# Two value projections done together, with some seven-product tile pairs, and the attention output held unsplit

## The chip, the cores and the metric

One core of one Trainium2 chip runs the whole program. The metric is the device time of one execution in microseconds (us); the time of a kernel is the median of several executions. Matrix products run on the tensor engine (PE); around it work the vector engine (DVE), the scalar engine (ACT), GpSimd (POOL) and a sync engine (SP) whose queue carries nearly all weight transfers. PE accumulates in eight banks of PSUM memory of 128 partitions x 512 floats.

## The reference

A decoder trunk on 256 tokens of width 2048, batch 1, two layers, all in float32:

```python
h = x
for layer in range(2):
    xn = rms_norm(h, attn_norm_g[layer])
    if layer == 0:                       # dilated sliding windows
        qkv = (xn @ w_qkv).reshape(b, s, 3, 3, 16, 128)   # group, q/k/v, head
        for g, (window, dilation) in enumerate(((128, 1), (512, 4), (2048, 16))):
            o_g, lse_g = window_attention(rope(q_g), rope(k_g), v_g)
        h = h + (sum_g softmax_g(lse)_g * o_g) @ w_o
    else:                                # latent attention on one shared K/V
        h = h + mla_attention(xn, k_nope, k_pe, v, ...)
    g, u = split(rms_norm(h, ffn_norm_g[layer]) @ w_gu)   # hidden width 5632
    h = h + (silu(g) * u) @ w_down
out = rms_norm(h, final_norm_g)
```

The change lies in the first layer's attention. It has 16 heads of 128; each head has a query, a key and a value for each of three groups, so the projection `w_qkv` has 2048 rows and 18432 columns. The mixture of the three groups is one softmax over the scores of all three together.

## The kernel before, in words

**Products.** A float32 product is made of three matmuls in a reduced-precision float32 form. Every operand is split into `hi` (the value rounded to that form, a copy on ACT) and `lo` (what is left, a subtraction on DVE); the product is hi x hi + hi x lo + lo x hi. Activations are held transposed, as 16 contraction tiles of 128 partitions with 256 columns of `hi` and 256 of `lo` for the tokens (`xT`). In `x_stationary` (L453) a 128-token half of x is loaded into PE and 512 columns of weights are streamed past it, three matmuls 128x512 a product. In `w_stationary` (L438) the weights are loaded and x is streamed.

**Weights.** All weights of the program are one list of units in the order of their use (`units`, from L294), mostly of 1 MB. `WeightStream` loads them through three `raw` buffers and splits each into `hi` and `lo` (three buffers each) two units ahead of the one in use: `next` (L195) issues the split of the unit two on, then loads. The forms "eight" and "seven" belong to a pair of contraction tiles times two blocks of 512 columns. Such a 2 x 2 product of blocks (two token halves x two contraction tiles x two column blocks) takes eight products; in the form "seven" it takes seven, from sums of blocks: four DVE operations on `raw` (L184 to L187) form sums of weights, split into `th` and `tl` (one buffer each), and the like sums of x are made once for all (`forms`, L655 to L664). The seven products go into the two accumulators of the column blocks and into four more banks (`pb`), which ACT and DVE join at the end (L704 to L711). Sums need x scaled by its token scale, or at least by a power of two near it, since the sums mix tokens.

**The feed-forward part** uses this for gate and up: `mixed` (L666) goes through eight pairs, of which `SEVEN = (2, 4, 6)` take seven products, except in each layer's first block of columns.

**The first attention** takes the heads in four quads. A quad projects values for its four heads, group by group, 16 products of contraction in four units each (L586; ACT takes the accumulator out with the token scale `rstd`, L590), and then, for two pairs of heads and three groups, the queries and keys (L597, two units each). `Later` (L203) holds work that is put some units ahead: scores come two units after their key (L604), and for a pair's last group the softmax of both its heads follows (L562 to L566); the values come three units after it (L605): PE transposes the softmax weights (L514), a copy brings them to `pt`, and four to six products with the values give the head's output (L572 to L578), which is split into `oT` right away (L581). So the second pair's softmax and values fall into the next quad's first value projection. A framework then orders the instructions of each engine by its own estimates, and each engine works through its list in order.

**Scales.** x is transposed with the layer's gain but without the token scale. The scale goes into the values as a column (`rstd`), into the softmax (`sc`, `nsc`), and into the keys as a row (`row_a["R"]`, L531). `across` (L423) makes such a row with one `diag` product on PE.

**Memory.** The pool `big` (L229) has two buffers of 4 MB; they hold in turn x, the transposed x (`xT_a`), the split output (`oT_a`) and the later stages' transposed activations.

## Time and profile before

| | |
|---|---|
| time, median of 3 runs | 2679.18 us (2678.85 to 2680.68) |
| profiled execution: time / span | 2679.5 us / 2677.7 us |
| mean granted PE clock | 0.999 of full |
| PE busy | 2661.3 us, 99% of the span, 12986 instructions |
| PE weight loads (overlap PE) | 2236.9 us, 84% |
| DVE busy | 1915.4 us, 72%, 2584 instructions |
| ACT busy | 1264.4 us, 47%, 1603 instructions |
| POOL busy | 5.5 us |
| read from memory | 491.57 MB, 184 GB/s over the span |

In the rows of the profile, an instruction is named by line, engine, operation and output <- inputs, with partitions x elements; a square bracket behind a row of the timeline gives the idle time of the engine just before it and what ended that. "PEld" is the loading of the stationary operand. The chain of waits is the work that ended last, followed back to the start.

### The profile page before, as it was taken

The numbers are of one execution on the slowest core, as the hardware profiler recorded it, in microseconds if no ns is written. First come the engines' busy times: TensorE is split into PE (matmuls) and PEld (weight loads), VectorE is DVE, ScalarE is ACT, GpSimd is POOL, SyncE is SP. The second block draws the span as 40 slices with busy tenths as digits, with TensorE's granted clock in tenths as the row PEclk, the third lists the DMA queues.
The fourth block names the chain that finished last, engine by engine and source line by source line (L and its number), as shares of the span: only waits on it lengthen the run. The fifth ranks groups of instructions, "written<-read, shape, count | busy, mean of one in ns | idle before, by whom it ended". The sixth has DMA issues, their size and how long they took to land.

```text
span 2677.7 us, 32660 instructions
## 1 busy us (share of the span) xinstructions
PE 2661.3 (99%) x12986; PEld 2236.9 (84%) x12986; DVE 1915.4 (72%) x2584; ACT 1264.4 (47%) x1603; POOL 5.5 (0%) x12
## 2 busy tenths in 40 slices
PE   9999999999999999999999999999999999999998
PEld 7888888888888888888888888888888888888887
DVE  5676577477467668966995796588578848984985
ACT  5444444444444445544553454565445534543553
POOL 0000000000000000000000000000000000000000
PEclk9999999999999999999999999999999999999999
DMA  7545555555555555565565655544555665655564
GB/s 272 189 160 171 189 165 168 186 173 173 173 183 164 195 182 189 189 204 189 189 219 190 204 180 197 161 140 146 174 173 189 205 198 179 219 190 194 191 217 138
DMA packets 302712, 495.78 MB, mean 185 GB/s; under 512 B 12680, under 2 KB 115808, under 8 KB 302176
## 3 DMA queue, kind: packets, MB, share of 16 engines
q1 hardware_dynamic: 301936, 492.64, 55.4%
q8 instruction: 101, 1.65, 0.3%
q10 hardware_dynamic: 624, 1.07, 0.1%
q14 instruction: 51, 0.42, 0.0%
HBM read 491.57 MB, written 2.10 MB: 184 GB/s over the span
## 4 chain that ended last, share of the span: by engine, by line
PE 95%; DVE 2%; DMA 1%; ACT 1%; issue 1%; SPq 0%; POOL 0%; POOLq 0%; DVEq 0%; ACTq 0%
PE acc L444 14%; PE acc L464 12%; PE acc L463 12%; PE acc L465 12%; PE acc L675 9%; PE acc L676 9%; PE acc L677 9%; PE acc L447 7%; PE bank L676 2%; PE bank L675 2%; PE bank L677 2%; PE bank L398 1%; PE bank L559 1%; DMA raw<-in_ffn_w_gu_dram 1%; PE bank L514 1%
## 5 line engine op out<-in xcount | busy, mean ns | idle before, releaser
L157 DVE TENSOR_TENSOR lo<-raw,hi 128x1024 fp32r<-128x1024 f32 (+2 forms) x578 | 667.5, 1179 | 464.2 <-ACT hi L156 447.9
L156 ACT CAST hi<-raw 128x1024 fp32r<-128x1024 f32 (+2 forms) x578 | 561.6, 1017 | 728.0 <-PE acc L465 312.1
L166 ACT CAST hi<-raw 128x1024 fp32r<-128x1024 f32 (+1 forms) x292 | 323.3, 1139 | 317.8 <-PE acc L677 96.3
L167 DVE TENSOR_TENSOR lo<-raw,hi 128x1024 fp32r<-128x1024 f32 (+1 forms) x292 | 383.4, 1330 | 83.5 <-ACT hi L166 82.8
L675 PE MATMUL acc<-hi,xT_f 128*128 128x512 f32 x988 | 387.2, 392 | 1.7 <-DVE gate L711 1.6
L676 PE MATMUL acc<-lo,xT_f 128*128 128x512 f32 x988 | 385.3, 390 | 0.0
L677 PE MATMUL acc<-hi,xT_f 128*128 128x512 f32 x988 | 385.2, 390 | 0.0
L444 PE MATMUL acc<-xT_a,hi 128*128 128x512 f32 x1536 | 379.3, 395 | 0.0
L444 PEld LDWEIGHTS acc<-xT_a,hi 128*128 128x128 f32 x1536 | 281.5, 188 | 53.8
L463 PE MATMUL acc<-hi,hT 128*128 128x512 f32 x704 | 274.7, 390 | 0.0
L465 PE MATMUL acc<-hi,hT 128*128 128x512 f32 x704 | 274.0, 389 | 0.0
L464 PE MATMUL acc<-lo,hT 128*128 128x512 f32 x704 | 274.0, 389 | 0.0
L675 PEld LDWEIGHTS acc<-hi,xT_f 128*128 128x128 f32 x988 | 185.5, 188 | 42.5 <-issue 2.9
L677 PEld LDWEIGHTS acc<-hi,xT_f 128*128 128x128 f32 x988 | 185.5, 188 | 39.3
L676 PEld LDWEIGHTS acc<-lo,xT_f 128*128 128x128 f32 x988 | 185.5, 188 | 38.4
L447 PEld LDWEIGHTS acc<-xT_a,lo 128*128 128x128 f32 x1536 | 196.9, 191 | 7.6
L447 PE MATMUL acc<-xT_a,lo 128*128 128x256 f32 x1536 | 199.2, 283 | 0.0
L166 ACT CAST th<-raw 128x1024 fp32r<-128x1024 f32 x120 | 121.8, 1049 | 73.1 <-DVE raw L186 64.6
L463 PEld LDWEIGHTS acc<-hi,hT 128*128 128x128 f32 x704 | 132.2, 188 | 27.6 <-issue 0.2
L465 PEld LDWEIGHTS acc<-hi,hT 128*128 128x128 f32 x704 | 132.1, 188 | 27.6
L464 PEld LDWEIGHTS acc<-lo,hT 128*128 128x128 f32 x704 | 132.2, 188 | 26.9
L464 PE MATMUL acc<-lo,xT_a 128*128 128x512 f32 x384 | 150.1, 391 | 0.8 <-DVE lo L157 0.6
(222 smaller groups left out, 3539.9 us busy)
## 6 DMA issues: line engine op xcount, KB each, us to landing
raw<-in_ffn_w_gu_dram SPq DMA_DIRECT2D x352, 512.0 KB, 4.5
raw<-in_a_w_qkv_dram SPq DMA_DIRECT2D x143, 1024.0 KB, 4.8
raw<-in_ffn_w_down_dram SPq DMA_DIRECT2D x88, 1024.0 KB, 5.1
raw<-in_a_w_o_dram SPq DMA_DIRECT2D x16, 1024.0 KB, 5.1
raw<-in_b_w_o_dram SPq DMA_DIRECT2D x16, 1024.0 KB, 5.0
raw<-in_b_w_kv_b_dram SPq DMA_DIRECT2D x8, 1024.0 KB, 5.2
raw<-in_b_w_q_b_dram SPq DMA_DIRECT2D x8, 768.0 KB, 4.8
raw<-in_b_w_q_a_dram SPq DMA_DIRECT2D x4, 1024.0 KB, 5.1
```

The costliest lines, as they stand in the source:

```text
L156: nc.scalar.copy(out=h, in_=src)
L157: nc.vector.tensor_tensor(out=l, in0=src, in1=h.bitcast(F32), op=ALU.subtract)
L166: self.nc.scalar.copy(out=hi, in_=src)
L167: self.nc.vector.tensor_tensor(out=lo, in0=src, in1=hi.bitcast(F32), op=ALU.subtract)
L444: mm(out=acc[:, i, :], lhsT=sl(hi, kk), rhs=xT[:, k0 + kk, :], start=first and kk == 0, stop=False)
L447: mm(out=acc[:, i, 0:S], lhsT=sl(lo, kk), rhs=xT[:, k0 + kk, 0:S], start=False, stop=last and kk == nk - 1)
L463: mm(out=acc[:, t, :ncol], lhsT=xh, rhs=rhs(hi, kk), start=st, stop=False)
L464: mm(out=acc[:, t, :ncol], lhsT=xh, rhs=rhs(lo, kk), start=False, stop=False)
L465: mm(out=acc[:, t, :ncol], lhsT=xl, rhs=rhs(hi, kk), start=False, stop=sp)
L675: mm(out=out, lhsT=xh, rhs=wh, start=st, stop=False)
L676: mm(out=out, lhsT=xh, rhs=wl, start=False, stop=False)
L677: mm(out=out, lhsT=xl, rhs=wh, start=False, stop=sp)
```

## The change

In quads 1, 2 and 3 the values of the first two groups are projected together by `mixed`, now a function of the whole kernel: eight units of two contraction tiles x two column blocks (one block a group), loaded by two transfers of 512 KB each in place of one of 1 MB, of which pairs 4 and 6 (`SEVEN_A`) take seven products. `mixed` returns the joined sums in `v0` and `v1`, which ACT then scales in place. Quad 0 and every third group keep their form.

For the sums, x is multiplied by a power of two of the token scale while quad 0 runs (`scaled`, eight operations in place on `xT_a`), and `rem_a`, the rest of the scale, takes the place of `rstd` behind that; the row for the keys is made a second time, from `rem_a`.

`th` and `tl` need memory in this stage too. So the two buffers of `big` become pools of their own: `big0` holds `xT_a`, and a pool `stage_a` holds x, `th` and `tl` until the attention is done; then `big1` opens. The split output has no buffer any more: heads 0 to 13 leave their output unsplit, by one ACT copy each, in the place of the untransposed x (`oT_f`), and four `output_parts` split it into the place of `xT_a` during and behind the last key product; heads 14 and 15 are split directly as before.

By the listed instructions, the program has 12667 matmuls and transposes in place of 12684: 18 fewer of 128x512, and one `diag` product more.

In the shortened `mixed`, the lines left out are those of the old one (L673 to L699) with `ga`, `ua` called `la`, `ra`.

```diff
 SEVEN = (2, 4, 6)
+SEVEN_A = (4, 6)
...
-        th, tl = [self.sum_pool.tile([P, 2048], F32R, tag=n, name=n, bufs=1) for n in ("th", "tl")]
+        th, tl = self.sum_tiles()
...
-    big = ctx.enter_context(tc.tile_pool(name="big", bufs=2))
+    bigs = [ctx.enter_context(tc.tile_pool(name="big0", bufs=1))]
...
+    stage_a = ExitStack()
+    a_pool = stage_a.enter_context(tc.tile_pool(name="stage_a", bufs=1))
+    def big_tile(i, shape, dtype, name):
+        return bigs[i].tile(shape, dtype, tag="big", name=name)
...
+    def paired(w, kp, at):
+        v = w.rearrange("(k p) c -> p k c", p=P)
+        return [v[:, 2 * kp:2 * kp + 2, b:b + 512] for b in at]
     for quad in range(HEADS // 4):
-        for g in range(NG):
+        if quad > 0:
+            at = [qkv_col(g, 2, quad * 4) for g in range(2)]
+            for kp in range(KD // 2):
+                units.append((paired(wq, kp, at), None, "seven" if kp in SEVEN_A else "eight"))
+        for g in range(NG) if quad == 0 else (2,):
...
-    xt = big_tile([P, NT, D], F32, "xt")
+    xt = a_pool.tile([P, NT, D], F32, name="xt")
+    oT_f = xt.rearrange("p t (h s) -> p (t h) s", s=S)
+    ws.sum_tiles = lambda: [a_pool.tile([P, 2048], F32R, tag=n, name=n) for n in ("th", "tl")]
...
+    def power_of_two(rstd):
+        r2, rem = [small.tile([P, NT], F32, tag=m, name=m) for m in ("r2", "rem")]
+        nc.vector.tensor_scalar(out=r2.bitcast(I32), in0=rstd.bitcast(I32), scalar1=0x7F800000,
+                                scalar2=None, op0=ALU.bitwise_and)
+        nc.vector.tensor_scalar(out=rem.bitcast(I32), in0=rstd.bitcast(I32), scalar1=0x007FFFFF,
+                                scalar2=0x3F800000, op0=ALU.bitwise_and, op1=ALU.bitwise_or)
+        return r2, rem
+    def scaled(xT, kp, R):
+        x2 = xT[:, 2 * kp:2 * kp + 2, :].rearrange("p k (h s) -> p k h s", s=S)
+        by = R.unsqueeze(1).unsqueeze(1).broadcast_to([P, 2, 2, S])
+        nc.vector.tensor_tensor(out=x2, in0=x2.bitcast(F32), in1=by, op=ALU.mult)
+    def sums(xT, kp, d):
+        x2 = xT[:, 2 * kp:2 * kp + 2, :].bitcast(F32)
+        f = tmp.tile([P, 2, S], F32, tag="t1", name="f")
+        nc.vector.tensor_tensor(out=f, in0=x2[:, :, 0:S], in1=x2[:, :, S:2 * S], op=ALU.add)
+        (a11, a21), (a12, a22) = [[f[:, k, t * P:(t + 1) * P] for t in range(NT)] for k in range(2)]
+        g = tmp.tile([P, 4, P], F32, tag="t1", name="g")
+        for i, x_, y_, op in ((0, a21, a22, ALU.add), (1, g[:, 0], a11, ALU.subtract),
+                              (2, a11, a21, ALU.subtract), (3, a12, g[:, 1], ALU.subtract)):
+            nc.vector.tensor_tensor(out=g[:, i], in0=x_, in1=y_, op=op)
+        put_split(d[:, 0], d[:, 1], g)
+    def mixed(xT, seven, forms, left, right, u2_tile):
+        la, ra = acc_tile(), acc_tile()
+        pb = None
...
+            if kp in seven:
+                i = seven.index(kp)
...
+                mul(pb[0], x(0, 0), w[:2], 1, st, sp)
...
+            later.tick()
+            if seven and kp == seven[-1]:
+                u2 = u2_tile()
+                nc.scalar.copy(out=left[:, 0], in_=pb[0])
+                for o, x_, y_ in ((u2, pb[2], left[:, 0]), (left[:, 1], pb[3], u2),
+                                  (right[:, 0], pb[1], u2), (right[:, 1], pb[1], left[:, 1])):
+                    nc.vector.tensor_tensor(out=o, in0=x_, in1=y_, op=ALU.add)
+        if not seven:
+            return la, ra
+        for acc, d in ((la, left), (ra, right)):
+            nc.vector.tensor_tensor(out=d, in0=acc, in1=d, op=ALU.add)
+        return left, right
...
     rstd = token_scale(ssq_x, "rstd")
+    r2_a, rem_a = power_of_two(rstd)
     row_a = {}
-    later.put(6, lambda: row_a.update(R=across(rstd, "R")))
+    later.put(6, lambda: row_a.update(R=across(r2_a, "R")))
     sc = small.tile([P, NT], F32, name="sc", tag="sc", bufs=1)
-    nc.vector.tensor_scalar(out=sc, in0=rstd, scalar1=P ** -0.5, scalar2=None, op0=ALU.mult)
+    nc.vector.tensor_scalar(out=sc, in0=rem_a, scalar1=P ** -0.5, scalar2=None, op0=ALU.mult)
     nsc = small.tile([P, NT], F32, name="nsc", tag="nsc", bufs=1)
-    nc.vector.tensor_scalar(out=nsc, in0=rstd, scalar1=-(P ** -0.5), scalar2=None, op0=ALU.mult)
-    oT = big_tile([P, HEADS, 2 * S], F32R, "oT_a")
+    nc.vector.tensor_scalar(out=nsc, in0=rem_a, scalar1=-(P ** -0.5), scalar2=None, op0=ALU.mult)
     swap = [(i + 16) % 32 for i in range(32)]
     with tc.tile_pool(name="attn_a", bufs=2) as ap:
         cst_a.append(ap.tile([P, C_END - C_M0], F32, name="cst_a", bufs=1))
         cos_a, sin_a = con(C_CA, S, A_ROT), con(C_SA, S, A_ROT)
+        forms_a = ap.tile([P, len(SEVEN_A), 2, 4, P], F32R, name="forms_a", bufs=1)
+        for kp in range(KD // 2):
+            later.put(7 + kp // 2, lambda kp=kp: scaled(xT, kp, row_a["R"]))
+        later.put(11, lambda: row_a.update(R=across(rem_a, "R")))
+        for i, kp in enumerate(SEVEN_A):
+            later.put(12 + i, lambda i=i, kp=kp: sums(xT, kp, forms_a[:, i]))
...
-            put_split(back(oT[:, head, 0:S]), back(oT[:, head, S:2 * S]),
-                      ot[:, :S].rearrange("p (t i) -> p t i", t=NT))
+            src = ot[:, :S].rearrange("p (t i) -> p t i", t=NT)
+            if head < HEADS - 2:
+                nc.scalar.copy(out=back(oT_f[:, head, :]), in_=src)
+            else:
+                put_split(back(oT[:, head, 0:S]), back(oT[:, head, S:2 * S]), src)
+        def output_parts(h0, h1):
+            put_split(oT[:, h0:h1, 0:S], oT[:, h0:h1, S:2 * S], oT_f[:, h0:h1, :])
         for quad in range(HEADS // 4):
-            vs = []
-            for g in range(NG):
-                acc = product(x_stationary, xT, KD)
-                v = ap.tile([P, NT, 512], F32, tag=f"v{g}", name=f"v{g}", bufs=1)
+            vs = [ap.tile([P, NT, 512], F32, tag=f"v{g}", name=f"v{g}", bufs=1) for g in range(NG)]
+            def put_v(v, acc, by):
                 for t in range(NT):
-                    nc.scalar.activation(out=v[:, t, :], in_=acc[:, t, :], func=AF.Copy, scale=rstd[:, t:t + 1])
-                vs.append(v)
+                    nc.scalar.activation(out=v[:, t, :], in_=acc[:, t, :], func=AF.Copy, scale=by[:, t:t + 1])
+            if quad > 0:
+                mixed(xT, SEVEN_A, forms_a, vs[0], vs[1],
+                      lambda: tmp.tile([P, 2, S], F32, tag="t1", name="u2").rearrange("p a b -> p (a b)"))
+                for v in vs[:2]:
+                    put_v(v, v, rem_a)
+            for g in range(NG) if quad == 0 else (2,):
+                put_v(vs[g], product(x_stationary, xT, KD), rem_a if quad > 0 or g == 2 else rstd)
             for pair in range(2):
                 st = {}
                 for g in range(NG):
                     qk = []
...
                     for which in range(2):
+                        if (quad, pair, g, which) == (HEADS // 4 - 1, 1, NG - 1, 1):
+                            oT = xT
+                            for h0 in (0, 4):
+                                later.put(1, lambda h0=h0: output_parts(h0, h0 + 4))
+                            for h0, h1 in ((8, 12), (12, HEADS - 2)):
+                                later.put(2, lambda h0=h0, h1=h1: output_parts(h0, h1))
                         acc = product(w_stationary, xT, KD, cols=(col(0), col(1)))
...
+    stage_a.close()
+    bigs.append(ctx.enter_context(tc.tile_pool(name="big1", bufs=1)))
...
+            def prepared(kp):
+                scaled(xT, kp, row["R"])
+                if kp in SEVEN:
+                    sums(xT, kp, forms[:, SEVEN.index(kp)])
             for part, (k0, n) in enumerate(FFN_PARTS):
                 last = part == len(FFN_PARTS) - 1
-                hT = big_tile([P, 16, 2 * S], F32R, "hT")
+                hT = big_tile(buf, [P, 16, 2 * S], F32R, "hT")
...
-                            later.put(kp + 3, lambda kp=kp: scaled(kp))
-                    g, u = mixed(not first, gate, up)
+                            later.put(kp + 3, lambda kp=kp: prepared(kp))
+                    g, u = mixed(xT, () if first else SEVEN, forms, gate, up,
+                                 lambda: fp.tile([P, 512], F32, tag="u2", name="u2"))
```

**First place: the start of the second quad's value projection**, where the first quad's last two heads have their softmax and values. On DVE, before, from the first head's softmax on (`sm` are the softmax weights, `sm_m` their row maxima, `sm_nb` the bias of the exponential, `sm_ri` the reciprocal of their sums, `pt` the transposed weights):

```order
L565 TENSOR_REDUCE sm_m<-mx 128x2
L157 TENSOR_TENSOR lo<-raw,hi 128x1024
L497 TENSOR_TENSOR sm_nb<-sm_m,nsc 128x2
L565 TENSOR_REDUCE sm_m<-mx 128x2
L497 TENSOR_TENSOR sm_nb<-sm_m,nsc 128x2
L504 RECIPROCAL sm_ri<-sm_rs 128x2
L506 TENSOR_SCALAR sm<-sm,sm_ri 128x512 x2
L516 COPY pt<-bank 128x512
```

The same stretch of DVE in the changed program (the rows of `raw` are the four sums of weights of pair 4):

```order
L662 TENSOR_REDUCE sm_m<-mx 128x2
L168 TENSOR_TENSOR lo<-raw,hi 128x1536
L586 TENSOR_TENSOR sm_nb<-sm_m,nsc 128x2
L662 TENSOR_REDUCE sm_m<-mx 128x2
L185 TENSOR_TENSOR raw<-raw 128x512
L586 TENSOR_TENSOR sm_nb<-sm_m,nsc 128x2
L186 TENSOR_TENSOR raw<-raw 128x512
L187 TENSOR_TENSOR raw<-raw 128x512
L593 RECIPROCAL sm_ri<-sm_rs 128x2
L188 TENSOR_TENSOR raw<-raw 128x512
L595 TENSOR_SCALAR sm<-sm,sm_ri 128x512 x2
```

Three of the four weight sums now stand ahead of the first head's reciprocal, and the fourth between it and the scaling of its weights. On PE there, before, at the transposes of the first head's weights:

```order
L463 MATMUL acc<-hi,xT_a 128x512
L514 MATMUL bank<-ident,sm 128x128 x2
L464 MATMUL acc<-lo,xT_a 128x512
L514 MATMUL bank<-ident,sm 128x128 x6
L465 MATMUL acc<-hi,xT_a 128x512
```

And in the changed program, up to the end of the transposes:

```order
L529 MATMUL acc<-hi,xT_a 128x512
L530 MATMUL acc<-lo,xT_a 128x512
L531 MATMUL acc<-hi,xT_a 128x512
L603 MATMUL bank<-ident,sm 128x128 x8
L529 MATMUL acc<-hi,xT_a 128x512
```

The eight transposes stand together, two matmuls later than the first of them stood before: 25 matmuls of the projection lie between them and the second head's scores, where it was 23.

**Second place: the end of the joint projection of groups 0 and 1**, DVE in the changed program (`u_2239` and `v_1917`, `v_1918` are the tile of the join and the two groups' values; `th`, `tl` and the `lo` ahead belong to pair 6):

```order
L168 TENSOR_TENSOR tl<-raw,th 128x1024 x2
L158 TENSOR_TENSOR lo<-raw,hi 128x1024 x3
L561 TENSOR_TENSOR u_2239<-bank,v_1917 128x512
L158 TENSOR_TENSOR lo<-raw,hi 128x1024
L561 TENSOR_TENSOR v_1917<-bank,u_2239 128x512
L561 TENSOR_TENSOR v_1918<-bank,u_2239 128x512
L561 TENSOR_TENSOR v_1918<-bank,v_1917 128x512
L565 TENSOR_TENSOR v_1917<-acc,v_1917 128x1024
L565 TENSOR_TENSOR v_1918<-acc,v_1918 128x1024
L158 TENSOR_TENSOR lo<-raw,hi 128x1024 x13
```

All of this is new here; before, DVE had nothing but `lo` rows, and the accumulators left by ACT (L590). Four `lo` of the third group's first two units stand ahead of the sums that end the join.

**Third place: the last key product of the attention**, DVE in the changed program (`qk` are keys, `sw` and `R` belong to their rotation and scale, `xT_a` is now the split output):

```order
L645 TENSOR_TENSOR qk_6948<-qk_6948,sw 32x512
L158 TENSOR_TENSOR lo<-raw,hi 128x1024
L388 TENSOR_TENSOR xT_a<-xt,xT_a 128x4x256 x2
L158 TENSOR_TENSOR lo<-raw,hi 128x1024 x2
L388 TENSOR_TENSOR xT_a<-xt,xT_a 128x4x256
L388 TENSOR_TENSOR xT_a<-xt,xT_a 128x2x256
L572 TENSOR_TENSOR qk_7046<-acc,t_7047 128x512
L158 TENSOR_TENSOR lo<-raw,hi 128x1024
L450 TENSOR_TENSOR qk_7046<-qk_7046,R 128x512
```

The four `xT_a` rows, the pieces of the output, are new; they stand ahead of the last key's evacuation (L572).

More of the change, by code (lines that the diff above doesn't have):

```diff
@@ L323, in units_ffn @@
         for k0, n in FFN_PARTS:
-            v = ffn_w_gu[layer].rearrange("(k p) c -> p k c", p=P)
             for j in range(k0, k0 + n, 4):
                 for kp in range(KD // 2):
-                    blocks = [v[:, 2 * kp:2 * kp + 2, b + j * P:b + j * P + 512] for b in (0, FF)]
-                    units.append((blocks, None, "seven" if j > 0 and kp in SEVEN else "eight"))
+                    units.append((paired(ffn_w_gu[layer], kp, (j * P, FF + j * P)), None,
+                                  "seven" if j > 0 and kp in SEVEN else "eight"))
             for c in range(0, D, 512):
```

118 lines of the change are left out of this document (39 added, 79 removed).

## The prediction

> **What bounds the kernel now.** I read the page's busy times and chain first, then the waits of the tensor engine, then the stretches of the first layer.
>
> ```profile
> span 2677.7 us, 32660 instructions
> PE 2661.3 (99%) x12986; PEld 2236.9 (84%) x12986; DVE 1915.4 (72%) x2584; ACT 1264.4 (47%) x1603; POOL 5.5 (0%) x12
> PE 95%; DVE 2%; DMA 1%; ACT 1%; issue 1%; SPq 0%; POOL 0%; POOLq 0%; DVEq 0%; ACTq 0%
> ...
> PE acc L675 <- DVE gate L711: 1.6, 2, 1.3
> ...
> 225.00:297.00 72.00, 71.99 (x338) 59.73 (x337) 37.42 (x53) 30.11 (x40) 0.00 (x0) 1.00 0.51 170
> ```
>
> PE is the bound: 95% of the chain, and its waits (microseconds in total, times, longest; the largest is shown) are crumbs. The last row is one stretch of value projections, the second quad's (length; then busy time and count for PE, PEld, DVE, ACT, POOL; the granted clock, here 1.00): PE 71.99 of 72.00, DVE 37.4. So the change is worth the PE work it removes, less any PE stall that it makes. There is no stall in that stretch to win back.
>
> **The work removed.** A pair of contraction tiles that took eight products takes seven; a product is three 128x512 matmuls. The feed-forward part does both forms already, so its rows price them:
>
> ```profile
> 1058.18 0.39 PE L675 MATMUL acc<-hi,xT_f 128*128 128x512 f32 x1
> 1063.42 0.39 PE L677 MATMUL acc<-hi,xT_f 128*128 128x512 f32 x1
> 1065.10 0.47 PE L675 MATMUL acc<-hi,xT_f 128*128 128x512 f32 x1 [1.29 <-DVE gate L711]
> 1076.99 0.39 PE L675 MATMUL bank<-hi,xT_f 128*128 128x512 f32 x1
> 1081.81 0.39 PE L675 MATMUL acc<-hi,xT_f 128*128 128x512 f32 x1
> ...
> 230.38 0.39 PE L463 MATMUL acc<-hi,xT_a 128*128 128x512 f32 x1
> 235.60 0.40 PE L465 MATMUL acc<-hi,xT_a 128*128 128x512 f32 x1
> ...
> L675 PEld LDWEIGHTS acc<-hi,xT_f 128*128 128x128 f32 x988 | 185.5, 188 | 42.5 <-issue 2.9
> ```
>
> First to last start of an eight-product tile pair is 5.24 us over 23 steps, 0.228 a matmul, so 24 take 5.47. A seven-product pair (the second block's first) runs from 1076.99 to 1081.81: 4.82. The difference is 0.65. In the first layer 24 matmuls start within 5.22 us, 0.227 each, so three are 0.68. Three quads with two such pairs each are 6 x 0.65 = 3.9 us, or 6 x 0.68 = 4.1 at best. I take 3.9.
>
> The Trainium skill ("TensorE: Matmul & The Clock Gate", section "Back-to-back issue gap") gives a stream of load and matmul pairs about 131 ns per 512-column matmul. By that 18 matmuls would be worth an estimated 2.4 us. The 0.227 of this trace decides, and the sum does not use the page's figure.
>
> **One matmul added.** The row form of the token scale is now built twice, first from the power of two, later from the rest. The trace has one such product:
>
> ```profile
> 39.34 0.39 PE L463 MATMUL acc<-hi,xT_a 128*128 128x512 f32 x1
> 40.02 0.60 PE L430 MATMUL bank<-diag,ones 128*128 128x256 f32 x2
> 41.15 0.39 PE L463 MATMUL acc<-hi,xT_a 128*128 128x512 f32 x1
> ```
>
> L463 comes every third matmul. From 39.34 to 41.15 are two threes, 6 x 0.227 = 1.36, so the product costs 0.45. The scaling of x itself is eight DVE instructions in the first quad (as L652), and the sums of each of the two tile pairs are two more of 512 columns and four of 128 (L186 has 512):
>
> ```profile
> L652 DVE TENSOR_TENSOR xT_f<-xT_f,R 128x1024 fp32r<-128x1024 f32 x16 | 19.6, 1224 | 10.9 <-PE acc L677 10.9
> L186 DVE TENSOR_TENSOR raw<-raw 128x512 f32<-128x512 f32 x60 | 41.4, 690 | 1.4
> ```
>
> At most 8 x 1.22 + 12 x 0.69 = 18 us, over eight weight tiles of 5.5 us in which the splits take two of 1.22 each: 38 of 44 us. Each scaling waits for the second group's last read of its tiles and has the length of two weight tiles until the third group's first. I put it at nothing; without that cover each late scaling would cost 1.22.
>
> **What DVE and ACT have to do more, and where.** Per quad, two weight tiles get the seven form:
>
> ```profile
> 1063.85 1.47 ACT L166 CAST hi<-raw 128x1536 fp32r<-128x1536 f32 x1 [4.07 <-PE acc L677]
> 1066.00 1.75 DVE L167 TENSOR_TENSOR lo<-raw,hi 128x1536 fp32r<-128x1536 f32 x1
> ...
> L167 DVE TENSOR_TENSOR tl<-raw,th 128x1024 fp32r<-128x1024 f32 x120 | 142.5, 1221 | 6.6 <-ACT th L166 6.2
> ```
>
> DVE: 1.75 + 4 x 0.69 + 2 x 1.22 = 6.9 us in place of 2.44, twice; then four sums of 0.69 and two of 1.22 to join the accumulators: 9.0 + 5.2 = 14 us on the 37.4 of 72. That fits on average; the place decides. The first seven-form split (pair 4) is due two tiles ahead, exactly when the preceding heads' softmax runs on DVE and ACT and PE wants its result:
>
> ```profile
> 236.03 2.00 ACT L156 CAST hi<-raw 128x1024 fp32r<-128x1024 f32 x2 [3.40 <-PE acc L465]
> 236.75 0.61 PE L559 MATMUL bank<-qk,qk 128*128 128x128 f32 x4
> 238.26 0.29 DVE L487 CUSTOM_DVE_ANT_0 sm<-bank,cst_a 128x128 f32<-128x128 f32 x1
> 239.88 0.16 DVE L497 TENSOR_TENSOR sm_nb<-sm_m,nsc 128x2 f32<-128x2 f32 x1
> 240.07 0.82 ACT L502 ACTIVATE sm<-sm,sm_nb,sc 128x512 f32<-128x512 f32 x1 [2.04 <-DVE sm_nb L497]
> 241.81 0.17 DVE L504 RECIPROCAL sm_ri<-sm_rs 128x2 f32<-128x2 f32 x1 [1.51 <-ACT sm L502]
> 242.01 0.88 DVE L506 TENSOR_SCALAR sm<-sm,sm_ri 128x512 f32<-128x512 f32 x2
> 242.55 0.44 PE L514 MATMUL bank<-ident,sm 128*128 128x128 f32 x2
> ```
>
> On this clock, with the changed order: ACT casts 1536 columns from 236.0 to 237.5. DVE, with no `lo` between the masks any more, has the second head's two (0.29 each, after the scores of 236.75) and the maximum done near 237.85, then the 1536-wide `lo` to 239.6, then the bias (0.3 earlier than now). So exp runs from 239.75, four of 0.8; its first pair ends at 241.4. But three of the four weight sums now stand ahead of the reciprocal and the fourth behind it: 239.7, 240.6, 241.3 and, after the reciprocal at 242.0, to 242.75. The first head's scaling then runs 242.75 to 243.6 instead of 242.01 to 242.89, 0.75 late. PE's transposes were put later too, behind 25 matmuls after the second scores instead of 23 (I count the order's rows), that is at 242.9. The second token half is wanted at about 243.0 and ready at 243.6: a stall of 0.6 us. Queued behind it on PE is the whole projection, so it counts in full. What follows is tight, not late: the first `pt` copy waits on ACT behind exp, `th` and the next `hi` (242.95 + 2.0 + 2.0 = 247.0) and ends by 247.8 even at the 0.82 of an exp; PE reaches it 15 matmuls after the transposes, near 247.8. `tl` of pair 4 is ready at 243.6 + 0.9 + 2.4 = 246.9, its use is past 255. Fewer changes between transposes and matmuls may give back 0.1. I take 0.5 per quad, 1.5 in all, between nothing and 1.2 per quad (the whole 0.75, and half a microsecond at the `pt` copies).
>
> **The end of the pair.** The two accumulators leave by DVE sums, and the third group's product needs the first one. The same structure in the feed-forward part cost once:
>
> ```profile
> 253.65 1.27 ACT L590 ACTIVATE v<-acc,rstd 128x512 f32<-128x512 f32 x2 [3.73 <-PE acc L465]
> ...
> 1057.78 2.00 ACT L166 CAST hi<-raw 128x1024 fp32r<-128x1024 f32 x2 [1.69 <-DMA raw<-in_ffn_w_gu_dram]
> 1058.87 1.23 DVE L167 TENSOR_TENSOR lo<-raw,hi 128x1024 fp32r<-128x1024 f32 x1 [1.53 <-ACT hi L166]
> 1063.73 1.23 DVE L711 TENSOR_TENSOR gate<-acc,gate 128x1024 f32<-128x1024 f32 x1
> ```
>
> The weight tile was late, everything behind it on DVE too, and PE stalled the 1.29 us quoted above; in 20 blocks it lost 1.6 in all by this. From the first `lo` after the wait to the end of the join are 6.1 us there. Here PE leaves the first four tiles at 253.6 (the row of L590) and half a microsecond of stall, 254.1. Pair 6 starts at 254.1 + 4.82 + 5.47 = 264.4; PE reaches `tl` nine matmuls on, at 266.45, and DVE has it near 265.4 (cast 254.1 to 255.6, `lo` to 257.4, the next tile's two `lo` and the four weight sums to 262.6, `tl` behind the casts of `th`). The cast of the second tile of the third group waits for pair 6's `hi` until 266.5 and for two ACT instructions before it, so its `lo` starts near 268.1 and the join ends near 274.2. PE wants it after pair 7, at 274.7. I take nothing, with 0 to 1.3 per quad as bounds.
>
> **The weight transfers and the output.** Eight transfers of 1024 KB per quad become sixteen of 512 KB on the same queue:
>
> ```profile
> raw<-in_ffn_w_gu_dram SPq DMA_DIRECT2D x352, 512.0 KB, 4.5
> raw<-in_a_w_qkv_dram SPq DMA_DIRECT2D x143, 1024.0 KB, 4.8
> ...
> 874.00 2.36 DVE L157 TENSOR_TENSOR lo<-raw,hi 128x1024 fp32r<-128x1024 f32 x2 [0.18 <-PE acc L447]
> 880.71 0.68 DVE L483 TENSOR_TENSOR qk<-acc,t 128x512 f32<-128x512 f32 x1
> 885.23 0.68 DVE L548 TENSOR_TENSOR qk<-qk,sw 32x512 f32<-32x512 f32 x1
> 890.23 0.61 PE L559 MATMUL bank<-qk,qk 128*128 128x128 f32 x4
> ```
>
> They land as soon, and the bytes are the same. The output of 14 heads is now one ACT copy per head, split late in four pieces into x's place. The first two pieces may start at 873.8, when PE leaves x's lower half: ACT to 876, DVE (behind the first `lo`) to 877.6, ahead of the use at 879.3. The other two wait until 879.3, take 1.6 us of ACT and 1.9 of DVE, and are needed at 890. They stand ahead of the last key's evacuation, which slides from 880.7 to 882.6; its rotation ends 5.2 later now, and there with one more `lo` of 1.2 between, near 889.1 against the scores at 890.23. Cover 1.1 us; cost nothing, and with the cover gone what exceeds it.
>
> **Sum.** 2679.5 (the profiled execution; its span is 2677.7) - 3.9 + 0.45 + 1.5 = 2677.55. That execution lies 0.3 above the median 2679.18, so the median comes to **2677.2**. The best bound, 4.1 saved and no stall, is -3.65: 2675.5. With all stall bounds it is -3.9 + 0.45 + 3 x (1.2 + 1.3) = +4.05: 2683.2.
>
> **Rivals.**
> *The order hides it all* (20%). For it: two-tile look-ahead, PE at 71.99 of 72. Against: the 0.75 us counted above. Time 2679.2 - 3.45 = 2675.7.
> *The accumulators leave late* (15%), the one on the other side. If a late weight tile holds DVE's in-order queue, the join ends after PE's last matmul of the pair. For it: the 1.29 stall, its row waiting for a transfer. Against: 2 stalls in 20 blocks. At 1.29 per quad beside the 0.5 it gives 2677.2 + 3.9 = 2681.1. Together with the values' stall it makes the change slower once a quad loses over 3.45 / 3 = 1.15 us. Were the second tile of the third group loaded into pair 6's buffer (in the built program it takes pair 7's, free near 260), it would land at 265.4 + 4.8 = 270.2, its `lo` start at 271.2 and the join end at 277.3: 2.6 of stall, three times, 2685.0.
> *The trade does not pay* (5%). Each removed matmul hides under the 0.188 of weight loading or the switches of bank cost as much as they save. Against: 4.82 against 5.47 us above. Time 2679.2 + 0.45 + 1.5 = 2681.1.
>
> **How the numbers follow.** My forecast of about -2 us holds 60%, with a range of its own of 2675.5 to 2679. The range 2674.8 to 2681.8 adds the hidden case with half a microsecond for the runs' spread, and most of the two slower ones; about 1 in 10 is left out above, less below. A measurement tells 0.2%, 5.4 us, from no change. Even the full 4.1 is below that, so faster by more needs a gain I do not see: 4%. Slower by more needs stalls of 8.8 us, close to 3 per quad, which only the worst of the second rival comes near: 6%. Within 0.2%: 90%.
>
> **What would show it.** The changed profile should have 17 matmuls fewer in the program; a seven-product pair in the first layer of 4.8 us beside 5.45; PE waits for the softmax scaling near 243, 460 and 679, some 0.3 to 0.8 us each; no wait for the joined accumulators, for `tl` or for the output's pieces; one more `diag` product near 68 us. A PE wait on the join or on `tl` of a microsecond or more in each quad would make the forecast wrong, as would a PE gap at 879.

## The result, and the profile after

The changed kernel took 2694.30 us (median of 6 runs, 2693.45 to 2695.14), the kernel before 2678.93 beside it: a ratio of 1.0056 (1.0045 to 1.0067), 15.4 us slower. The forecast was 2677.2, in a range of 2674.8 to 2681.8.

The page of the changed kernel, its span, its busy times and the chain by engine:

```profile
span 2692.3 us, 32776 instructions
PE 2677.6 (99%) x12970; PEld 2235.9 (83%) x12970; DVE 1966.3 (73%) x2644; ACT 1279.2 (48%) x1621; POOL 5.5 (0%) x12
PE 97%; DVE 1%; DMA 1%; ACT 1%; issue 0%; SPq 0%; POOL 0%; POOLq 0%; DVEq 0%; ACTq 0%
```

PE has 16 recorded instructions fewer than before and is busy 16.3 us longer, at a granted clock of 0.999 as before. The waits of PE (total, times, longest) are as small as before, and none is new:

```profile
PE acc L529 <- DVE gate L565: 1.5, 2, 1.0
PE bank L255 <- DVE mhalf L381: 1.1, 1, 1.1
PE bank L412 <- DMA xt<-in_x_dram: 0.8, 1, 0.8
PE acc L458 <- ACT vb L906: 0.7, 1, 0.7
```

So the time is in the matmuls themselves. By stage, from the first matmul of one to the first of the next (of the last stage, to the start of its last matmul), in us:

| stage | before | after |
|---|---|---|
| first attention, from its first product | 968.30 | 965.58 |
| feed-forward of layer 0 | 716.19 | 723.92 |
| latent projections from `xT_b` | 53.03 | 54.20 |
| latent attention | 113.78 | 113.44 |
| its output product (`oT_b`) | 96.64 | 98.82 |
| feed-forward of layer 1 | 713.58 | 720.03 |

The stage that was changed is 2.7 us faster. All the loss is in stages whose program is the old one. Two stretches of 60 us in down projections, layer 0 and layer 1, the instructions on `hT` alone (busy us and counts of PE, PEld, DVE, ACT); before:

```profile
1160.00:1220.00 60.00, 60.00 (x266) 49.69 (x265) 0.00 (x0) 0.00 (x0) 1.00 0.60 194
2150.00:2210.00 60.00, 60.00 (x267) 49.67 (x266) 0.00 (x0) 0.00 (x0) 1.00 0.60 195
```

and after:

```profile
1160.00:1220.00 60.00, 60.00 (x266) 49.70 (x265) 0.00 (x0) 0.00 (x0) 1.00 0.60 194
2150.00:2210.00 60.00, 60.00 (x259) 48.31 (x258) 0.00 (x0) 0.00 (x0) 1.00 0.58 192
```

The same product with nothing on DVE or ACT that touches `hT`: 266 matmuls in 60 us in layer 0, 259 in layer 1, at a full clock (the 1.00 in the row). Gate and up in layer 0 show it too. Two matmuls of the timeline 24 apart, before and then after:

```profile
989.45 0.39 PE L675 MATMUL acc<-hi,xT_f 128*128 128x512 f32 x1
994.89 0.39 PE L675 MATMUL acc<-hi,xT_f 128*128 128x512 f32 x1
```

```profile
989.79 0.40 PE L531 MATMUL acc<-hi,xT_f 128*128 128x512 f32 x1
995.39 0.40 PE L531 MATMUL acc<-hi,xT_f 128*128 128x512 f32 x1
```

That is 5.44 / 24 = 0.2267 us a matmul before and 5.60 / 24 = 0.2333 after. The slow products are those of `xT_f` in layer 0, `xT_b`, `oT_b` and `hT` in layer 1: 1572 + 192 + 384 + 1056 = 3204 matmuls of 128x512. What they share is the buffer of their stationary operand, the second one of 4 MB. The change made it a pool of its own, opened behind the pools that serve the whole program. It holds the stationary operand; the moving one is `hi` or `lo`. The byte addresses in a partition of SBUF, as the two programs have them:

```
                         before    after
first big buffer          22016    22016
second big buffer         54784   135968
hi (first of three)      112128    79360
lo (first of three)      136704   103936
forms (feed-forward)     185120   185120
th (feed-forward)        205600   205600
```

Before, both big buffers, `hi` and `lo` are a multiple of 512 bytes apart. After, the second big buffer lies 56608 = 110 x 512 + 288 behind the first `hi`.

### The profile page after: what moved, and what is told of

Its sections match the earlier page's. It is cut to its first block, busy times and chain, and to the rows that moved or that the text cites. A ratio compares the mean times of both kernels' runs of the same rounds, so it can differ in the third digit from the quotient of the medians.

```text
span 2692.3 us, 32776 instructions
## 1 busy us (share of the span) xinstructions
PE 2677.6 (99%) x12970; PEld 2235.9 (83%) x12970; DVE 1966.3 (73%) x2644; ACT 1279.2 (48%) x1621; POOL 5.5 (0%) x12
## 4 chain that ended last, share of the span: by engine, by line
PE 97%; DVE 1%; DMA 1%; ACT 1%; issue 0%; SPq 0%; POOL 0%; POOLq 0%; DVEq 0%; ACTq 0%
PE acc L458 14%; PE acc L529 11%; PE acc L530 11%; PE acc L531 11%; PE acc L479 11%; PE acc L478 11%; PE acc L477 11%; PE acc L461 7%; PE bank L529 2%; PE bank L530 2%; PE bank L531 2%; PE bank L412 1%; PE bank L656 1%; PE bank L603 1%; PE bank L671 1%; DMA raw<-in_ffn_w_gu_dram 1%
## 5 line engine op out<-in xcount | busy, mean ns | idle before, releaser
L158 DVE TENSOR_TENSOR lo<-raw,hi 128x1024 fp32r<-128x1024 f32 (+2 forms) x530 | 610.4, 1175 | 394.0 <-ACT hi L157 368.0
L157 ACT CAST hi<-raw 128x1024 fp32r<-128x1024 f32 (+2 forms) x530 | 513.3, 1013 | 647.0 <-PE acc L458 261.9
L167 ACT CAST hi<-raw 128x1024 fp32r<-128x1024 f32 (+1 forms) x334 | 367.8, 1134 | 388.0 <-PE acc L531 124.4
L168 DVE TENSOR_TENSOR lo<-raw,hi 128x1024 fp32r<-128x1024 f32 (+1 forms) x334 | 436.9, 1326 | 119.6 <-ACT hi L167 118.3
L167 ACT CAST th<-raw 128x1024 fp32r<-128x1024 f32 x132 | 133.7, 1048 | 84.4 <-DVE raw L187 76.2
L168 DVE TENSOR_TENSOR tl<-raw,th 128x1024 fp32r<-128x1024 f32 x132 | 156.7, 1220 | 7.9 <-ACT th L167 7.5
```

The lines of the kernel that those rows point to most:

```text
L157: nc.scalar.copy(out=h, in_=src)
L158: nc.vector.tensor_tensor(out=l, in0=src, in1=h.bitcast(F32), op=ALU.subtract)
L167: self.nc.scalar.copy(out=hi, in_=src)
L168: self.nc.vector.tensor_tensor(out=lo, in0=src, in1=hi.bitcast(F32), op=ALU.subtract)
```

## The experiments

**Multiples of 64 bytes.** The first theory was that the two operands of a matmul must start alike within 64 bytes: the second buffer had moved from a multiple of 64 to 32 past one. A tile of a few bytes, made longer, moves all that lies behind it, and the order of the instructions stays. e1 and e3 have this edit, in the changed kernel and in the one before:

```diff
-    nsc = small.tile([P, NT], F32, name="nsc", tag="nsc", bufs=1)
+    nsc = small.tile([P, 10], F32, name="nsc", tag="nsc", bufs=1)[:, :NT]
```

> The changed kernel with one small tile made 32 bytes longer, so that every tile behind it in SBUF starts at a multiple of 64 bytes instead of 32 bytes past one: among them the second 4 MB buffer, th, tl and forms. Order of instructions and everything else are the same. Theory (a 128x512 matmul takes 233 ns instead of 227 when its stationary and its moving operand start at different offsets within 64 bytes): the feed-forward part of layer 0, the latent attention's products and the last down projections go back to 227 ns a matmul; 14.7 us of loss vanish, and the forms' products of all seven-product pairs gain 2 x 180 x 6.7 ns = 2.4 us more. 2674 us, between 2672.5 and 2676. Rival (the second buffer is slow because of where it lies, behind all the other pools, not because of 32 bytes): no change, 2694. Rival (the other order of DVE and ACT work takes PE's time): no change, 2694.

> The kernel before with the same small tile made longer, so that forms, th and tl (and all that lies behind) start at a multiple of 64 bytes like hi, lo and xT. Theory of the two offsets: six matmuls of each of the 60 seven-product pairs go from 233 to 227 ns: 2.4 us less, 2676.8, between 2676 and 2678. Rivals (place or order): no change, 2679.2.

e2 moves the second buffer by 32 bytes. The two longer slots also move `forms`, `th` and `tl` of the feed-forward parts, by 64 bytes, from 32 to 96 bytes past a multiple of 256; by the theory of 64 that changes nothing:

```diff
+        if i == 1:
+            t = bigs[1].tile([P, 8 + KD * 2 * S], dtype, tag="big", name=name)
+            return t[:, 8:].rearrange("p (k s) -> p k s", s=2 * S)
-    h = hpool.tile([P, NT, D], F32, name="h")
+    h = hpool.tile([P, 8 + NT * D], F32, name="h")[:, 8:].rearrange("p (t d) -> p t d", d=D)
```

> The changed kernel with only the second 4 MB buffer moved up by 32 bytes, to a multiple of 64; th, tl, forms, and all the rest stay 32 bytes past one. Theory of the two offsets: the time goes to what the prediction summed, without stalls: 2676.5 us, between 2675.5 and 2678; the second layer's and first layer's feed-forward matmuls at 227 ns, those of forms with hi and of xT with th at 230 to 233 as before the change. Rival (place, or order of DVE and ACT): no change, 2694.

e4 moves everything large in the kernel before by 32 bytes:

```diff
-    mhalf = cpool.tile([P, NT], F32, name="mhalf")
+    mhalf = cpool.tile([P, 10], F32, name="mhalf")[:, :NT]
```

> The kernel before with another small tile made longer, ahead of everything large: both 4 MB buffers, raw, hi and lo now start 32 bytes past a multiple of 64, and forms, th and tl at a multiple. So xT, hT, hi and lo are all off, but off alike. Theory of two different offsets: what counts is that the two operands agree, so the time stays as before, 2679.2, between 2678 and 2681. Rival (each operand that starts off a multiple of 64 costs by itself): about 10000 matmuls at 6.7 ns more, 2740 or above.

Measured, with the kernel before at 2678.29: e1 2691.95, e2 2695.48, e3 2676.09, e4 2679.38. e1 and e2 missed what was expected by 18 and 19 us; e3 and e4 came out as expected. The theory falls: at a multiple of 64 the second buffer is as slow as ever. The stretch of e1 in layer 1's down projection, as above:

```profile
2150.00:2210.00 60.00, 60.00 (x259) 48.35 (x258) 0.00 (x0) 0.00 (x0) 1.00 0.57 187
```

But 32 bytes did change what lies with `forms` and `th` (e1 and e3 each gained 2.2 to 2.4 us), and in e4, where all of them moved alike by 32 bytes, the time stayed: an operand's own address did not count there. That leaves the distance between the two operands, with 64 as the wrong number.

**The distance by itself.** e5 is nothing but matmuls, in one execution, 32 for each distance, with the stationary operand at a varied place (`o` counts 4 bytes; `W` and `X` start 2048 bytes apart, which is left out of the distances):

```
offs = list(range(0, 128, 4)) + list(range(128, 512, 16)) + [1024, 2048, 4096, 8192, 16384]
for o in offs:
    acc = ps.tile([P, 512], F32, name="acc", tag="acc")
    for i in range(32):
        mm(out=acc, lhsT=X[:, o:o + P], rhs=W, start=i == 0, stop=i == 31)
```

> Only matmuls of the kernel's kind, all on zeros, with no other work beside them; the layer's computation is left out. For each of 61 distances between the start of the stationary operand (128 columns, 512 bytes a partition) and that of the moving one (512 columns) 32 matmuls 128x512 in a row: distances in steps of 16 bytes up to 512, then of 64 up to 2048, then 4, 8, 16, 32 and 64 KB. Theory (what costs is the distance between the two operands, modulo 512 bytes: the loading of the next stationary operand and the stream of the moving one meet in the same part of SBUF): 227 ns a matmul at distance 0 and at each multiple of 512, about 233 ns at 288 and 320 bytes, and the same pattern in each stretch of 512 bytes. Rival (distance doesn't matter; the second buffer's rows are slow for another cause, such as the copies on DVE and ACT beside them): 227 ns at every distance.

Windows that reach from the first start of one group of 32 to the first start of the next, at distances 0, 32, 256, 288, 320 and 512 (their length is the reading; then PE and PEld):

```profile
13.00:20.25 7.25, 7.25 (x33) 6.01 (x32) 0.00 (x0) 7.25 (x5) 0.00 (x0) 1.00 0.00 0
27.52:34.97 7.45, 7.45 (x33) 6.01 (x32) 0.00 (x0) 0.00 (x0) 0.00 (x0) 1.00 0.00 0
131.72:138.97 7.25, 7.25 (x33) 6.01 (x32) 0.00 (x0) 0.00 (x0) 0.00 (x0) 1.00 0.00 0
146.24:153.69 7.45, 7.45 (x33) 6.01 (x32) 0.00 (x0) 0.00 (x0) 0.00 (x0) 1.00 0.00 0
161.16:168.62 7.46, 7.46 (x34) 6.01 (x32) 0.00 (x0) 0.00 (x0) 0.00 (x0) 1.00 0.00 0
250.44:257.69 7.25, 7.25 (x33) 6.01 (x32) 0.00 (x0) 0.00 (x0) 0.00 (x0) 1.00 0.00 0
```

7.25 / 32 = 226.6 ns, 7.45 / 32 = 232.8. The mean gap of the last 16 matmuls of each group, from the starts in the trace, by distance modulo 256 bytes:

```
  0: 226.7   16: 226.7   32: 233.3   48: 233.3   64: 233.3   80: 231.9   96: 234.1  112: 233.3
128: 233.4  144: 233.3  160: 233.6  176: 230.0  192: 233.3  208: 233.4  224: 233.3  240: 226.6
```

The second 256 bytes repeat the first within 0.1 ns. From 512 to 2048, in steps of 64, the multiples of 256 are as 0 again, 64 beyond them is 233.3 and 128 beyond 232.9; only 192 beyond is less than in the first 256 bytes, 228.9. The distances of 4 to 64 KB are as 0. So the rival of e5 is out: the cost needs no DVE, no ACT and no transfer. (ACT still makes copies in the first window, and its 7.25 is that of 256 and 512 without them.) The theory is right in kind, and the period is 256, not 512. By itself e5 varies only the stationary operand's place. But its moving operand starts at 128 modulo 256, that of the kernel at 0 and that of e4 at 32, and in each the fast place is where the two agree; so it is the distance. In this map 32 (the changed kernel, 288) and 64 (e1, e2) cost the same, which is why 32 bytes more did nothing for the second buffer.

The gain of e1 and e3 is not in this map, since `forms` and `th` went from 32 to 64 there too. A seven-product pair of the feed-forward part and the twelve matmuls behind it take 7.57 us in the kernel before, 7.53 in e3 and 7.48 in e8 below; 0.04 us for 60 pairs is 2.4 us, near the 2.2 that e3 gained. e5 has 32 matmuls in a row at one distance, the pair has three. Why 64 costs less than 32 in so short a row stays open.

**The changed kernel, with its operands at one place.** e6 is e1's edit with `P, 64` for `P, 10` (224 bytes): the second buffer, `th`, `tl` and `forms` come to multiples of 512. e7 is e2's with 56 and 72 floats for 8: the second buffer moves by 224 bytes, and `forms`, `th` and `tl` by 512, which leaves their distances modulo 256 as they were. e8 is e3 with `P, 64`.

> The changed kernel with one small tile made 224 bytes longer, so that the second buffer, th, tl and forms start at a multiple of 512 bytes, as hi, lo and xT do. Theory of distance modulo 512: all products at 227 ns; 2670 us, between 2668.5 and 2672. Rival (the place of the second buffer, or other work): 2691 to 2695, as with multiples of 64.

> The changed kernel with only the second 4 MB buffer moved up by 224 bytes, to a multiple of 512; forms, th and tl stay at 288 modulo 512 as before the change. Theory of distance: the mean matmul of the first feed-forward part back from 234 to 228 ns, and the time to what the change itself is worth: 2675.7 us, between 2674.5 and 2677. Rival (place or other work): 2694.

> The kernel before with one small tile made 224 bytes longer, so that forms, th and tl start at a multiple of 512. Theory of distance modulo 512: the excess over 226.7 ns a matmul in and behind each of the 60 seven-product pairs, 86 ns a pair, goes: 5.2 us less, 2673.1, between 2672 and 2675. Rival (multiples of 64 are all that counts): as with these, 2676.1.

Measured, with the kernel before at 2678.31: e6 2670.33, a ratio of 0.9970 (0.9958 to 0.9981); e7 2675.45, 0.9990 (0.9981 to 0.9999); e8 2673.98, 0.9984 (0.9975 to 0.9993). All three are what the distance says. e6's stretches in both down projections:

```profile
1160.00:1220.00 60.00, 60.00 (x266) 49.70 (x265) 0.00 (x0) 0.00 (x0) 1.00 0.60 197
2150.00:2210.00 60.00, 60.00 (x266) 49.70 (x265) 0.00 (x0) 0.00 (x0) 1.00 0.58 193
```

From after to e7 is 18.85 us, 5.9 ns for each of the 3204 matmuls. That is a net: in the changed kernel `xT_f` of layer 0 and `th` agreed (both at 32 modulo 256, by the addresses above), and in e7 they no longer do.

**The loss without the change.** e10 starts each big buffer of the kernel before 288 bytes late, in a slot as much longer, so that the first one ends up at a distance of 224 from `hi` and `lo`, and the second at 0:

```diff
-        return big.tile(shape, dtype, tag="big", name=name)
+        t = big.tile([P, 72 + KD * 2 * S], dtype, tag="big", name=name)[:, 72:]
+        if len(shape) == 2:
+            return t[:, :shape[1]]
+        return t[:, :shape[1] * shape[2]].rearrange("p (k s) -> p k s", s=shape[2])
```

> The kernel before, with both 4 MB buffers begun 288 bytes later in slots that are 288 bytes longer. The second buffer then lies at the same place modulo 256 as hi and lo, the first at 224. So the attention output, the first layer's down projections and the second layer's gate and up (384 + 1056 + 1572 matmuls) have their stationary operand at a distance of 224, nothing else of the program is changed. Theory of distance: the same sort of loss as the change had, at the 5.9 ns a matmul by which the changed kernel's 3204 such matmuls (1572 + 192 + 384 + 1056) differ between it and e7: 17.7 us, 2696, between 2692 and 2700. Rival (the loss needs something that the change brought): 2678.5.

Measured 2697.94 (two executions) beside 2679.40: 18.5 us lost, 17.7 expected. Now it is layer 0's down projection that is slow:

```profile
1166.00:1226.00 60.00, 60.00 (x259) 48.20 (x258) 0.00 (x0) 0.00 (x0) 1.00 0.60 192
```

The expectation overlooks that `ccT`, the latent attention's operand, lies in the first buffer too. Its products, 160 of 512 columns and 160 + 192 of 256, also came to a distance of 32 or 224, and lost nothing: the latent attention took 113.41 us in e10 and 113.78 in the kernel before, and the 192 follow each other at 117 ns in e10 where it was 120.

**What the removed products are worth, and the period in the kernel.** e9 takes e6 and gives all pairs of the first layer eight products; e11 has the small tile at `P, 128`, so that the moved tiles lie at 256 modulo 512.

```diff
-SEVEN_A = (4, 6)
+SEVEN_A = ()
-                mixed(xT, SEVEN_A, forms_a, vs[0], vs[1],
+                got = mixed(xT, SEVEN_A, forms_a, vs[0], vs[1],
-                for v in vs[:2]:
-                    put_v(v, v, rem_a)
+                for v, acc in zip(vs[:2], got):
+                    put_v(v, acc, rem_a)
```

> The kernel of e6 (all operands at multiples of 512 bytes) with eight products in every tile pair of the first layer: the joint projection of groups 0 and 1, the scaling of x, the unsplit output and all the rest stay, the accumulators go straight to ACT. Theory: each of the six pairs takes 24 matmuls of 226.7 ns again in place of 21, 4.08 us in all, so 2674.4, between 2673.3 and 2675.5, close to e8 (2674.0), since the other parts of the change cost next to nothing. Rival (the other parts cost or gain a microsecond or more, hidden in the sum): off 2674.4 by that much.

> The kernel of e6 with the small tile 256 bytes longer still: the second buffer, th, tl and forms lie at 256 modulo 512. Theory of a period of 256 bytes, as the stretch of matmuls alone shows it: as e6, 2670.3, between 2669 and 2671.5. Rival (it is 512 bytes that count in the kernel): products of x with hi and lo slow again, 2688 or above.

Measured 2679.50 and 2674.43, with the kernel before at 2679.40 on this chip: 4 to 5 us above what was expected, and e11 short of its rival's 2688. Part of the excess is in the waits of PE for joined accumulators in the feed-forward parts: 5.2 us in e11 (its rows are shown) and 3.7 in e9, where e6 had 1.6:

```profile
PE acc L529 <- DVE gate L565: 4.4, 4, 1.9
PE acc L477 <- DVE gate L565: 0.8, 3, 0.4
```

e12 to e15 are the kernels of e6, e11, e9 and e8 again, side by side on one chip:

> The kernel of e6 once more, on the same chip as e13, e14 and e15, since e9 and e11 were taken on another chip than e6 and e8, and lay 4 to 5 us above what was forecast. Theory (those 4 to 5 us are late weight transfers in the feed-forward parts, which differ from chip to chip and execution to execution): this one lies within 1 us of e13. Its distance to the kernel before is 6.5 to 9 us.

> The kernel of e11 (second buffer, th, tl, forms at 256 modulo 512) on the same chip as e12. Period of 256 bytes: within 1 us of e12, in the stretch of the first attention within 0.5 us. Rival (512 bytes count to a small extent): 2 to 4 us above e12.

> The kernel of e9 (all operands at multiples of 512 bytes, eight products in every tile pair of the first layer) on the same chip as e12. Theory: 4.0 us above e12 (six pairs of 0.67 us), by the first attention's stretch; if e9's excess was transfers, no more than 1 us beside that. Rival (the removal of products is worth more for another reason): 7 us or more above e12.

> The kernel of e8 (the kernel before with forms, th and tl at multiples of 512 bytes) on the same chip as e12. Theory: 3.5 us above e12, of it 4.0 from the seven-product pairs less 0.45 of the second diag product; within 1 us of e14.

Measured, with the kernel before at 2678.21: e12 2670.28 (0.9971, 0.9959 to 0.9982), e13 2670.95, e14 2675.61, e15 2673.54. e13 is within 0.7 us of e12, so 256 bytes are the period in the kernel too, and e11's excess is not of the distances; that it was late transfers, as e12's expectation has it, is not shown. e14 lies 5.3 above e12, where 4.0 was expected. The traces, whose spans are 5.8 apart, have 4.06 in the three quads' value stretches (72.03 each in e14, 70.68, 70.66 and 70.68 in e12). The rest is 1.1 more before the first quad's keys, 1.8 less in layer 0's feed-forward, 1.9 more in layer 1's (711.43 against 709.57) and 0.8 more behind the last matmul (in e9 too); neither edit touches the feed-forward parts. e14 against e15 is 2.1, where less than 1 was expected; the second `diag` product explains 0.46 (see below), and the first quad's keys begin at 81.37 in e14 and 79.65 in e15. They begin anywhere from 78.98 to 81.08 in six profiles of the kernel before and its moved forms, so this part stays open.

e6 and e12, the change with one small tile 224 bytes longer, beat both kernels: 8.0 and 7.9 us under the kernel before.

## Why the prediction was wrong

Point by point, in its order.

**PE is the bound, and there is no stall to win back: right.** Before and after, PE's waits are crumbs.

**The removed work: right in kind, 3.5 where I took 3.9.** A quad's value stretch went from 72.05 to 70.89 us, in each of the three quads, 1.16 for two pairs, net of whatever else moved in it. The second seven-product pair of the second quad, its first matmul and the first behind its end:

```profile
265.12 0.39 PE L529 MATMUL bank<-hi,xT_a 128*128 128x512 f32 x1
269.94 0.39 PE L529 MATMUL acc<-hi,xT_a 128*128 128x512 f32 x1
```

4.82, as in the feed-forward part. But I priced only the 21 matmuls. Those of `forms` with `hi` and of `xT` with `th` are at a distance, and the gaps stay long for a few matmuls behind the pair. With all operands at one place (e6) the two pairs take 4.79 and 4.76, the quad 70.70, and two pairs save 1.34: 0.67 each, between my 0.65 and the 0.68 I called the best.

**One matmul added, 0.45: right.** The changed kernel's second row product stands near 69 us:

```profile
68.31 0.39 PE L477 MATMUL acc<-hi,xT_a 128*128 128x512 f32 x1
69.00 0.60 PE L444 MATMUL bank<-diag,ones 128*128 128x256 f32 x2
70.13 0.39 PE L477 MATMUL acc<-hi,xT_a 128*128 128x512 f32 x1
```

From 68.31 to 70.13 are six matmuls of the projection, 1.36 us at 0.2267, so the product costs 0.46. The start of the first quad's keys is too scattered to show it: 80.4 on average in ten profiles with the change or part of it, 80.1 in six without, within a spread of 2 us.

**The softmax stall of 0.5 per quad: a miss.** The order was as printed, the wait was not. The changed kernel at the second quad's start (its clock is 1.36 us later than that of before there):

```profile
240.90 0.82 ACT L591 ACTIVATE sm<-sm,sm_nb,sc 128x512 f32<-128x512 f32 x1 [2.04 <-DVE sm_nb L586]
...
242.90 0.16 DVE L593 RECIPROCAL sm_ri<-sm_rs 128x2 f32<-128x2 f32 x1
243.01 0.69 DVE L188 TENSOR_TENSOR raw<-raw 128x512 f32<-128x512 f32 x1
...
243.62 0.87 DVE L595 TENSOR_SCALAR sm<-sm,sm_ri 128x512 f32<-128x512 f32 x2
...
244.26 1.17 PE L603 MATMUL bank<-ident,sm 128*128 128x128 f32 x8
```

All as I had it: the weight sums around the reciprocal, the scaling behind the fourth, PE at 242.9 on the old clock. But exp began at 239.54 instead of 239.75, the reciprocal came at 241.54 instead of 242.0, and the scaling ended at 243.1 instead of 243.6. In the starts of the eight transposes two gaps are longer than the usual 109 ns, 188 and 165: 0.14 us. My sum had exp 0.2 us too late, the reciprocal 0.46 and the scaling's end 0.5, which is the whole stall. The other two quads' transposes show the same two gaps.

**The join, `tl`, the first quad's scaling, the output pieces at nothing: right.** No such wait is among those of the page, and from the last quad's first key to the feed-forward part it is 242.48 before and 242.53 after. One small gain stood in no term: the third quad's keys take 145.88 us where it was 146.34, and so in every profile of either order (146.27 to 146.34 in six, 145.9 to 146.0 in ten). Its cause was not tested.

**What failed is the sum itself: it had no term for where the tiles lie.** I listed instructions removed, added and moved, and their waits. The opening of `big1` behind the other pools I took for bookkeeping, and the 0.227 us of a matmul for a constant of the whole program. By e5 that pace holds only at a distance of 0 modulo 256 bytes, or within 16 of it, and is 0.233 at most others. The 17.2 us by which the stages behind the first attention are longer are this (with the second buffer put back, in e7, the feed-forward of layer 0 is at 716.17 again and `oT_b` at 96.59); 2.5 fewer before them, and the span is 14.6 longer. No rival had it: all three looked at waits and at the products themselves. With only the second buffer put back (e7), the change is worth 2.86 us beside its own kernel before, against the 2.0 that I forecast; the interval of that run, 0.3 to 5.1 us, does not tell the two apart. The value stretches do: they are 3.5 us shorter in all, where my sum had 3.9 less 1.5 of stall, 2.4. So the mechanism that I forecast was there and a little larger than forecast, and the loss beside it came from a term that was not in the sum.

The row that could have told me was among those I quoted. Matmuls of `xT_f` with `hi` follow each other at 0.2267, and 21 of them would take 4.76. The seven-product pair took 4.82, and behind it the gaps were long again, with PE waiting for nothing: 86 ns a pair, 5.2 us for 60 pairs. I used the 4.82 and did not ask why it was not 4.76.

## What to carry to other kernels

Where PE is the bound with 512-column matmuls back to back, each with its own load, the distance in SBUF between stationary and moving operand is worth a look before any wait: print the addresses, and keep buffers that meet in a product a multiple of 256 bytes apart (here within 16 bytes of it). A pool that is moved, split or opened later moves everything behind it, and a change that only touches one stage can slow others whose instructions are the same; stage lengths, and matmuls per window in a stage that was not changed, show it at once. A price taken from a row holds for the place of the operands in that row.

## What the runs showed of the hardware

A stream of 128x512 matmuls, each with its own load of 128 columns, ran at 226.7 ns a matmul where the two operands' start addresses agree modulo 256 bytes within 16, and at 229 to 234 ns elsewhere, 2.9% more at most places (e5). It needs no other engine's work. The pace settles after a change of distance: at 240 bytes the first eight gaps of e5's group have 229.1 on average, the last sixteen 226.6. The Trainium skill ("TensorE: Matmul & The Clock Gate", section "Step-by-step: what each phase is for") says that the engine has two independent read ports of SBUF, and that loading the next weights takes no read bandwidth from the running matmul. The map of e5 does not agree with independence: only the place of one operand against the other was varied, and the pace changed. Whether the two reads meet in one part of the memory, as the period of 256 bytes suggests, or something else depends on the distance, no run here tells. Products of other shapes were not mapped, and the one case of them shows no cost: the 256-column matmuls of `ccT` in e10, at a distance of 224, were no slower than at 0 (117 ns against 120).
